# Both branches' first score chunk in one product, and squares summed by ScalarE, in a two-layer decoder trunk

## The chip, the cores and the metric

The kernel runs on one core of one Trainium2 chip. The metric is the device time of one execution in microseconds (us). The profile below is of one execution taken by the hardware profiler; PE is TensorE (PEld its weight loads), ACT is ScalarE, DVE is VectorE, POOL is GpSimd, SP is SyncE, which issues most DMAs.

## What is computed

Two layers over 512 positions of width 1024, all in float32. Layer 0 has one input projection whose columns feed an mLSTM branch (4 heads of 128) and a sparse attention branch (8 query heads of 64 in 2 key/value groups), then one output projection. Layer 1 is a gated linear recurrence (HGRN2, 8 heads of 128) between two projections. Cut to what the change touches:

```python
qh = partial_rope(rms_norm(heads(q, 8), q_norm), pos) * (64 ** -0.5)
ks_h = partial_rope(rms_norm(heads(ks, 2), k_norm[1]), pos)      # selected branch
kw_h = partial_rope(rms_norm(heads(kw, 2), k_norm[2]), pos)      # window branch
...
s_s = q . ks ;  p_s = masked_softmax(s_s) ; o_s = p_s @ vs       # with 8 blocks and top-k 16, all causal keys
s_w = q . kw ;  p_w = masked_softmax(s_w) ; o_w = p_w @ vw       # the window of 512 spans the sequence
out = g0 * o_c + g1 * o_s + g2 * o_w
...
h = rms_norm(h_mlstm, head_norm)      # mLSTM: mean of squares per head of 128
o = rms_norm(o_hgrn2, head_norm)      # HGRN2: the same
```

So the selected and the window branch are both plain causal attention of the same queries over different keys and values, and every head norm needs a sum of squares.

## The kernel before, in words

**Layout.** The 512 positions are four chunks of 128 (`NT = 4`). Large projections run as three products for each float32 one (the high and low parts of both operands, `whi`/`wlo` against `h0h`/`h0l`): ACT rounds a weight block into `whi` and DVE subtracts to give `wlo` (`cvt_w`). These products are the dense work; each streams 512 columns.

**Order.** The code describes work in strands (generators) that a small flow model interleaves in program order: `dense0` and `dense1` go through the projection groups and have the lowest priority, the others (`prep_q`, `prep_k`, `nsa_a`, `nsa_b`, `m_head`, `m_tok`, `hgrn`) are put between their products as their inputs come ready. Then `Plan` takes all operations of a layer with a price for each and places them again by a list schedule (six rounds, the best kept), on all engines. So whatever changes an operation, its price or its buffers changes the order written to every queue. Work buffers come in rings; the tag `big` has 5 (`BB`), counted by `hb(n)` (wait until n are free) and `b_end()` (give one back).

**Queries and keys (`prep_q`, `prep_k`, one call each per chunk).** From the projected rows `qk[i]` (8 heads of q, then 4 of k, 64 columns each) ACT squares all heads in one instruction into `sq`, a block of the tag `big`; POOL multiplies `qk[i]` by the norm weight in place; DVE sums each head's 64 squares (`tensor_reduce` into `qss` or `kss4`); POOL makes the reciprocal root in two instructions (`rsqrt_mean`); DVE scales into `x2` and applies the rotation; PE transposes; ACT and DVE write the high and low parts stacked on the partitions (`q2`) or side by side (`kd[g][:, c, br, :]`, c for high and low, br for the branch).

**Scores (`nsa_a`).** There are 16 units: for each group, pair of heads and branch br (0 selected, 1 window), two heads hh. A unit goes through the four query chunks i: two products (c = 0, 1) of the same queries as weights against `128 * (i + 1)` key columns, into one bank of the tag `sc` (two banks); DVE adds the causal mask and takes the minimum into `nm`; ACT takes the exponential into the unit's row block `PP` with the row sum into `sm`. Then DVE scales each chunk's block by gate over sum. `nsa_b` transposes the blocks on PE (`tp<-cs,PP` in the profile) and multiplies with the values.

**Head norms.** In `m_tok` (4 calls) and in `hgrn` (8 calls) ACT squares four blocks of 128 columns, one instruction each with the sum in `accum_out`. All four write their squares, which nobody reads, to the same scrap block `hj`.

In the profile a matmul is named by output, then moving and weight operands; an ACT instruction with `accum_out` is followed by an ACTIVATION_READ_ACCUMULATOR. All operations are recorded by one helper, so all rows have the line L408 and are told apart by tile names; `x` there is the tile `x2`, `kss` is `kss4`, `krs` is `krs4`, `hj` is also the second layer's `hj1`, and `CUSTOM_DVE_ANT_0` is the masking minimum.

Of the kernel before, what the change touches and what calls it, by code (L numbers as in the profile page):

```python
# [31 lines left out]
NT = 4  # L32
# [583 lines left out]
def build(tc, I, out):  # L616
# [6 lines left out]
    with ExitStack() as ctx:  # L623
# [323 lines left out]
        with ExitStack() as c0:  # L947
# [8 lines left out]
            def hb(n):  # L956
                return lambda: big[0] >= n
# [4 lines left out]
            def b_t(name, shape, dt=F32):  # L962
                big[0] -= 1
                assert big[0] >= 0, name
                return cut(sp.tile([128, 1280], dt, name=name, tag="big", bufs=BB), shape)
# [238 lines left out]
            def turn(x2):  # L1204
# [3 lines left out]
                return cut(p, (4, 128))  # L1208

            def prep_q(i):  # L1210
                yield hb(2)
                x = qk[i][:, :8, :]
                ts_ = slice(128 * i, 128 * (i + 1))
                sq = b_t("sq", (8, 64))
                A.activation(sq, x, AF.Square)
                P.tensor_tensor(x, x, cust(qnB, [[0, 8], [1, 64]]), op=OP.mult)
                ss = s_t("qss", [128, 8])
                V.tensor_reduce(ss, sq, axis=AX.X, op=OP.add)
                b_end()
                rq = s_t("qrs", [128, 8])  # L1220
# [18 lines left out]
            def prep_k(i):  # L1239
                yield hb(2)  # L1240
                x = qk[i][:, 8:, :]
                ts_ = slice(128 * i, 128 * (i + 1))
                sq = b_t("sq", (4, 64))
                A.activation(sq, x, AF.Square)
                P.tensor_tensor(x.rearrange("p (a b) c -> p a b c", a=2), x.rearrange("p (a b) c -> p a b c", a=2),
                                cust(knB, [[64, 2], [0, 2], [1, 64]], 64), op=OP.mult)
                ss = s_t("kss4", [128, 4])
                V.tensor_reduce(ss, sq, axis=AX.X, op=OP.add)
                b_end()
                rk = s_t("krs4", [128, 4])  # L1250
# [55 lines left out]

            def nsa_a():
                yield [E("q%d" % i) for i in range(4)] + [E("k%d" % i) for i in range(4)] + [E("gt")]
                for u, (g, pr, br, hh) in enumerate(UN):
                    hg = 4 * g + 2 * pr + hh  # L1310
                    yield [hb(1), lambda u=u: ndone[0] >= u - 1, SCS]
                    pp = b_t("PP", (1280,))
                    nm = s_t("nm", [128, 4], 3)
                    sm = s_t("sm", [128, 4], 3)
                    for i in range(NT):
                        n = 128 * (i + 1)
                        yield SCS
                        s = sc_t()
                        for c in range(2):
                            T.matmul(s[:, :n], q2[g][:, hh, pr, 128 * i:128 * (i + 1)], kd[g][:, c, br, :n],  # L1320
                                     start=c == 0, stop=c == 1)
                        V.tensor_tensor_reduce(s[:, :n], s[:, :n], cz[:, 512 - n:], 1.0, -NEG, op0=OP.add, op1=OP.min,
                                               accum_out=nm[:, i:i + 1])
                        A.activation(pp[:, OFF[i]:OFF[i] + n], s[:, :n], AF.Exp, bias=nm[:, i:i + 1], scale=-1.0,
                                     accum_out=sm[:, i:i + 1])
                    V.reciprocal(sm, sm)
                    V.tensor_tensor(sm, sm, cust(gt, [[24, 4]], 3 * hg + 1 + br), op=OP.mult)
                    for i in range(NT):
                        sl = slice(OFF[i], OFF[i] + 128 * (i + 1))
                        V.tensor_scalar(pp[:, sl], pp[:, sl], sm[:, i:i + 1], None, op0=OP.mult)  # L1330
                    PPs[u] = pp
                    fl.mark(E("A%d" % u))
                    if u % 8 == 7:
                        u_end(1 + u // 8)
# [3 lines left out]
            def nsa_b():  # L1338
                pts = []
                yp = None  # L1340
                for u, (g, pr, br, hh) in enumerate(UN):
                    yield [E("A%d" % u), hb(1)]
                    pp = PPs.pop(u)
                    ptl = b_t("PT", (1280,))
                    m = []
                    for kbs, o in (((0,), 0), ((1,), 512), ((2, 3), 896)):
# [3 lines left out]
                        for kb in kbs:  # L1350
                            for i in range(kb, NT):
                                T.transpose(tp[:, c:c + 128], pp[:, OFF[i] + 128 * kb:OFF[i] + 128 * (kb + 1)], idf)
                                c += 128
# [133 lines left out]
            def m_tok(t):  # L1487
# [21 lines left out]
                hs = s_t("hs", [128, 4])  # L1509
                hj = s_t("hj", [128, 128], 1)  # L1510
                for h in range(4):
                    A.activation(hj, nd[:, h, :128], AF.Square, scale=rd[:, h:h + 1], accum_out=hs[:, h:h + 1])
                hr = s_t("hr", [128, 4])
# [204 lines left out]
        with ExitStack() as c1:  # L1718
# [60 lines left out]
            def hgrn(h):  # L1779
# [100 lines left out]
                hs = s_t("hs1", [128, 4])  # L1880
                hj = s_t("hj1", [128, 128], 1)
                for t in range(4):
                    A.activation(hj, op[:, 128 * t:128 * (t + 1)], AF.Square, accum_out=hs[:, t:t + 1])
                hr = s_t("hr1", [128, 4])
# [234 lines left out]
```

## Time and profile before

| | before |
|---|---|
| median of three runs | 623.28 us (620.89 to 623.8) |
| the profiled execution | 619.54 us, its span 617.8 us |
| PE busy | 609.2 us (99%) |
| DVE busy | 463.9 us (75%) |
| ACT busy | 326.4 us (53%) |
| POOL busy | 104.5 us (17%) |
| mean granted TensorE clock | 0.997 of full |

Busy time is the share of the span in which an engine had an instruction; matmuls are pipelined and the profile models their ends, so what one of them costs is read from the distance between starts, not from its duration. A timeline merges neighbours of the same kind (x2). In brackets behind a row stands the idle time of the engine before it and what ended it.

### The profile page before, as it was taken

What the parts mean: (1) busy time and instruction counts of PE and PEld (TensorE: products, weight loads), DVE (VectorE), ACT (ScalarE), POOL (GpSimd) and SP (SyncE); (2) the same over time, 40 slices, a digit from 0 to 9 for tenths busy, and PEclk for the clock granted to TensorE, in tenths of its full rate; (3) what the DMA queues carried; (4) which work ended last, traced back from release to release, by engine and by line L of the source; (5) the groups of instructions that cost most, each with busy time, mean ns of one, the idle gap of its engine ahead of it and who ended that gap; (6) DMA issues with size and microseconds to landing.
All of it is one profiled execution on the core that took longest, in us unless ns stands there. A gap on an engine that the chain in (4) does not pass through costs nothing.

```text
span 617.8 us, 11670 instructions
## 1 busy us (share of the span) xinstructions
PE 609.2 (99%) x4498; PEld 492.0 (80%) x4498; DVE 463.9 (75%) x988; ACT 326.4 (53%) x778; POOL 104.5 (17%) x131
## 2 busy tenths in 40 slices
PE   8999998999999999999999999999999999999997
PEld 8877886877777777888888887788877877788886
DVE  5888989988899875656746669997688798986441
ACT  7554433675676765273534757447527375565410
POOL 1424252031100000063003111023000100122100
PEclk9998999999999999999999999999999999999999
DMA  8823137679994004016244424473222215473111
GB/s 293 278 117 103 51 103 256 203 164 342 247 203 138 0 2 147 7 46 228 77 162 136 154 85 138 118 240 121 69 72 69 70 34 173 138 282 128 35 69 68
DMA packets 23526, 82.90 MB, mean 134 GB/s; under 512 B 3376, under 2 KB 4272, under 8 KB 20656
## 3 DMA queue, kind: packets, MB, share of 16 engines
q1 hardware_dynamic: 21168, 65.39, 32.2%
q0 software_dynamic: 2304, 16.78, 10.3%
q8 instruction: 35, 0.57, 0.4%
q14 instruction: 19, 0.16, 0.1%
HBM read 77.96 MB, written 20.97 MB: 160 GB/s over the span
## 4 chain that ended last, share of the span: by engine, by line
PE 92%; DVE 3%; DMA 1%; issue 1%; POOL 1%; ACT 1%; SPq 0%; ACTq 0%; DVEq 0%
PE mm L408 35%; PE mx L408 17%; PE my L408 15%; PE sc L408 8%; PE tp L408 5%; PE ac L408 5%; PE tq L408 5%; PE sd L408 2%; DMA raw<-in_wall_dram 1%; DVE wlo L408 1%; DVE HB L408 0%; DVE AL L408 0%; POOL krs L408 0%; ACT whi L408 0%; DVE x L408 0%
## 5 line engine op out<-in xcount | busy, mean ns | idle before, releaser
L408 ACT ACTIVATE whi<-raw 128x512 fp32r<-128x512 f32 (+1 forms) x184 | 105.0, 614 | 76.2 <-PE my L408 29.5
L408 DVE TENSOR_TENSOR wlo<-raw,whi 128x1024 fp32r<-128x1024 f32 (+1 forms) x96 | 114.7, 1202 | 20.4 <-ACT whi L408 20.1
L408 PE MATMUL mm<-whi,h0h 128*128 128x512 f32 (+1 forms) x168 | 68.2, 407 | 0.0
L408 PE MATMUL mm<-whi,h0l 128*128 128x512 f32 (+1 forms) x168 | 67.9, 405 | 0.0
L408 PE MATMUL mm<-wlo,h0h 128*128 128x512 f32 (+1 forms) x168 | 67.4, 405 | 0.0
L408 ACT ACTIVATE PP<-sc,nm 128x128 f32<-128x128 f32 (+2 forms) x64 | 33.7, 527 | 26.0 <-DVE nm L408 22.9
L408 DVE CUSTOM_DVE_ANT_0 sc<-sc,cz 128x128 f32<-128x128 f32 (+2 forms) x64 | 31.4, 502 | 11.7 <-PE sc L408 9.1
L408 PE MATMUL mm<-h0h,whi 128*128 128x512 f32 x96 | 39.5, 411 | 0.0
L408 PE MATMUL mm<-h0h,wlo 128*128 128x512 f32 x96 | 38.1, 397 | 0.6 <-DVE wlo L408 0.6
L408 PE MATMUL mm<-h0l,whi 128*128 128x512 f32 x96 | 38.6, 402 | 0.0
L408 PEld LDWEIGHTS mm<-whi,h0l 128*128 128x128 f32 x168 | 32.1, 192 | 5.8 <-issue 0.2
L408 PEld LDWEIGHTS mm<-wlo,h0h 128*128 128x128 f32 x168 | 32.2, 192 | 5.6 <-issue 0.2
L408 PEld LDWEIGHTS mm<-whi,h0h 128*128 128x128 f32 x168 | 32.3, 192 | 5.2
L408 DVE TENSOR_TENSOR HB<-HB,tt 128x512 f32<-128x512 f32 x48 | 31.9, 687 | 4.4 <-PE sd L408 3.1
L408 PE MATMUL sc<-kd,q 128*128 128x512 f32 (+3 forms) x128 | 31.3, 330 | 0.0
L408 ACT ACTIVATE PT<-tp 128x384 f32<-128x384 f32 (+1 forms) x48 | 24.0, 526 | 9.5 <-PE tp L408 9.2
L408 POOL TENSOR_TENSOR ivgg<-ivgg,zz 128x256 f32<-128x256 f32 x16 | 17.8, 1116 | 65.9 <-ACT zz L408 65.9
L408 POOL TENSOR_SCALAR hr<-hs 128x4 f32<-128x4 f32 x12 | 2.3, 193 | 142.7 <-ACT hj L408 142.6
L408 PE MATMUL tp<-cs,PP 128*128 128x128 f32 x160 | 26.3, 275 | 0.0
L408 PEld LDWEIGHTS sc<-kd,q 128*128 128x128 f32 x128 | 22.7, 191 | 4.0 <-ACT PT L408 0.8
L408 PE MATMUL my<-h1l,whi 128*128 128x512 f32 x64 | 25.8, 403 | 0.0
L408 PE MATMUL mx<-h1l,whi 128*128 128x512 f32 x64 | 25.8, 402 | 0.0
(374 smaller groups left out, 1556.7 us busy)
## 6 DMA issues: line engine op xcount, KB each, us to landing
raw<-in_wall_dram SPq DMA_DIRECT2D x76, 512.0 KB, 3.8
wt<-in_wall_dram POOLq DMA_DIRECT2D x12, 1024.0 KB, 14.2
raw<-wt SPq DMA_DIRECT2D x16, 512.0 KB, 3.7
wt<-wt POOLq DMA_DIRECT2D x4, 1024.0 KB, 22.7
bias<-in_brow_dram SPq DMA_DIRECT2D x9, 256.0 KB, 4.1
xt<-in_xt_dram SPq DMA_DIRECT2D x8, 256.0 KB, 5.4
w<-in_cw_dram SPq DMA_DIRECT2D x2, 1024.0 KB, 9.4
x<-in_xt_dram SPq DMA_DIRECT2D x2, 1024.0 KB, 6.8
```

Source lines behind the costliest of these rows:

```text
L408: o.fn(*o.a, **k)
```

## The change

Three edits. **Scores:** in `nsa_a` the first chunk (128 keys) of both branches is computed in the unit of branch 0: its two products stream 256 columns (`kd[g][:, c, :, :128]`), DVE and ACT treat the two halves of the bank one after the other, and the window branch's half goes to a tile `e0` (128 columns, three buffers) and to that unit's own `nm1`/`sm1`. The units of branch 1 start at chunk 1. **Squares of q and k:** in place of one ACT instruction over all heads and a DVE reduction, ACT squares one head at a time with `accum_out`, into a scrap tile `sqj` with one block for each head; `sq` and its block of the tag `big` go away, and the strand waits for one free block and not two. **Head norms:** the four squares go to four blocks of a scrap tile (`sqj` in `m_tok`, `hj1` of four times the size in `hgrn`).

```diff
+            def squares(x, ss):
+                j = cut(s_t("sqj", [128, 512], 1), (8, 64))
+                for a in range(x.shape[1]):
+                    A.activation(j[:, a, :], x[:, a, :], AF.Square, accum_out=ss[:, a:a + 1])
             def prep_q(i):
-                yield hb(2)
+                yield hb(1)
...
-                sq = b_t("sq", (8, 64))
-                A.activation(sq, x, AF.Square)
+                ss = s_t("qss", [128, 8])
+                squares(x, ss)
                 P.tensor_tensor(x, x, cust(qnB, [[0, 8], [1, 64]]), op=OP.mult)
-                ss = s_t("qss", [128, 8])
-                V.tensor_reduce(ss, sq, axis=AX.X, op=OP.add)
-                b_end()
                 rq = s_t("qrs", [128, 8])
...
(prep_k: the same with 4 heads)
...
                     pp = b_t("PP", (1280,))
-                    nm = s_t("nm", [128, 4], 3)
-                    sm = s_t("sm", [128, 4], 3)
-                    for i in range(NT):
+                    if br == 0:
+                        for b_ in range(2):
+                            mm_[b_, hh] = s_t(f"nm{b_}", [128, 4], 3), s_t(f"sm{b_}", [128, 4], 3)
+                        first[hh] = s_t("e0", [128, 128], 3)
+                    nm, sm = mm_[br, hh]
+                    def chunk(s, n, i, p, nm, sm):
+                        V.tensor_tensor_reduce(s, s, cz[:, 512 - n:], 1.0, -NEG, op0=OP.add, op1=OP.min,
+                                               accum_out=nm[:, i:i + 1])
+                        A.activation(p, s, AF.Exp, bias=nm[:, i:i + 1], scale=-1.0, accum_out=sm[:, i:i + 1])
+                    for i in range(br, NT):
...
                         for c in range(2):
-                            T.matmul(s[:, :n], q2[g][:, hh, pr, 128 * i:128 * (i + 1)], kd[g][:, c, br, :n],
-                                     start=c == 0, stop=c == 1)
...
+                            T.matmul(s[:, :n] if i else cut(s, (2, 128)), q2[g][:, hh, pr, 128 * i:128 * (i + 1)],
+                                     kd[g][:, c, br, :n] if i else kd[g][:, c, :, :n], start=c == 0, stop=c == 1)
+                        chunk(s[:, :n], n, i, pp[:, OFF[i]:OFF[i] + n], nm, sm)
+                        if i == 0:
+                            chunk(s[:, 128:256], n, i, first[hh], *mm_[1, hh])
...
-                hj = s_t("hj", [128, 128], 1)
+                hj = cut(s_t("sqj", [128, 512], 1), (4, 128))
                 for h in range(4):
-                    A.activation(hj, nd[:, h, :128], AF.Square, scale=rd[:, h:h + 1], accum_out=hs[:, h:h + 1])
+                    A.activation(hj[:, h, :], nd[:, h, :128], AF.Square, scale=rd[:, h:h + 1], accum_out=hs[:, h:h + 1])
...
-                hj = s_t("hj1", [128, 128], 1)
+                hj = s_t("hj1", [128, 4, 128], 1)
                 for t in range(4):
-                    A.activation(hj, op[:, 128 * t:128 * (t + 1)], AF.Square, accum_out=hs[:, t:t + 1])
+                    A.activation(hj[:, t, :], op[:, 128 * t:128 * (t + 1)], AF.Square, accum_out=hs[:, t:t + 1])
```

The rest of the diff takes the first block of a branch 1 unit from `e0` where DVE scales it and PE transposes it.

## Rows read from the trace of the kernel before

**Rows 1.** The page, its first part: busy time of the engines, its share of the span, and the number of instructions.

```profile
PE 609.2 (99%) x4498; PEld 492.0 (80%) x4498; DVE 463.9 (75%) x988; ACT 326.4 (53%) x778; POOL 104.5 (17%) x131
```

**Rows 2.** The page's chain of work that ended last, by engine, as shares of the span.

```profile
PE 92%; DVE 3%; DMA 1%; issue 1%; POOL 1%; ACT 1%; SPq 0%; ACTq 0%; DVEq 0%
```

**Rows 3.** Busy time by stretch: the stretch and its length, then PE, PEld, DVE, ACT and POOL, each with its number of instructions, the granted clock, and the DMA's share and rate. From 36 to 104 us q and k are prepared, from 104 to 235 us `nsa_a` runs, up to 345 us the last projections of layer 0, from 410 to 520 us most of `hgrn`.

```profile
36.00:104.00 68.00, 66.09 (x375) 53.10 (x374) 59.09 (x142) 26.84 (x62) 27.00 (x30) 0.97 0.31 103
...
50.50:54.00 3.50, 3.50 (x10) 2.85 (x10) 2.90 (x7) 0.00 (x0) 0.00 (x0) 0.51 0.11 16
104.00:235.00 131.00, 131.00 (x731) 100.96 (x731) 110.67 (x316) 88.10 (x228) 11.40 (x16) 1.00 0.59 161
235.00:345.00 110.00, 110.00 (x544) 90.17 (x543) 65.21 (x107) 51.61 (x123) 22.71 (x23) 1.00 0.35 117
410.00:520.00 110.00, 109.05 (x1241) 87.43 (x1243) 89.96 (x193) 60.75 (x153) 13.99 (x19) 1.00 0.29 92
```

**Rows 4.** The waits of PE over the span: who waited for whom, us in total, times, the longest.

```profile
PE tp L408 <- DVE kd L408: 1.2, 1, 1.2
...
PE mm L408 <- DVE wlo L408: 0.6, 1, 0.6
...
PE tq L408 <- DVE yo L408: 0.2, 1, 0.2
```

**Rows 5.** Groups of PE instructions with shapes kept apart: the scores' first chunk, its count, busy time and mean duration.

```profile
L408 PE MATMUL sc<-kd,q 128*128 128x128 f32 x32 | 6.6, 267 | 0.0
```

**Rows 6.** The timeline of PE in the scores, where a first and a second chunk of one unit stand between dense products: start, duration.

```profile
110.65 0.33 PE L408 MATMUL sc<-kd,q 128*128 128x128 f32 x2
110.82 0.45 PE L408 MATMUL mm<-h0l,whi 128*128 128x512 f32 x1
111.11 0.39 PE L408 MATMUL mm<-h0h,wlo 128*128 128x512 f32 x1
111.34 0.39 PE L408 MATMUL mm<-h0h,whi 128*128 128x512 f32 x1
...
111.81 0.40 PE L408 MATMUL sc<-kd,q 128*128 128x256 f32 x2
112.05 0.40 PE L408 MATMUL mm<-h0h,wlo 128*128 128x512 f32 x1
112.28 0.39 PE L408 MATMUL mm<-h0h,whi 128*128 128x512 f32 x1
```

**Rows 7.** The tile `sq` from 36 to 96 us: count, shortest, median and longest duration in ns, first and last start.

```profile
L408 ACT ACTIVATE sq<-qk x8: 409/520/632, 37.3 to 90.0; 128x512 f32<-128x512 f32 x4, 128x256 f32<-128x256 f32 x4
L408 DVE TENSOR_REDUCE qss<-sq x4: 668/676/680, 42.4 to 64.5; 128x8 f32<-128x512 f32 x4
L408 DVE TENSOR_REDUCE kss<-sq x4: 405/412/420, 76.9 to 93.9; 128x4 f32<-128x256 f32 x4
```

**Rows 8.** The timeline of ACT at the one square of 64 columns with a sum that the kernel before has (64 partitions).

```profile
47.65 0.26 ACT L408 ACTIVATE kn<-kr 64x64 f32<-64x64 f32 x1 [1.20 <-DVE kr L408]
47.82 0.19 ACT L408 ACTIVATION_READ_ACCUMULATOR kn<-kr 64x1 f32 x1
```

**Rows 9.** The timeline of ACT at two exponentials of a unit in a row: they write different blocks of the tile `PP` and different columns of `sm`.

```profile
107.49 0.37 ACT L408 ACTIVATE PP<-sc,nm 128x128 f32<-128x128 f32 x1 [0.43 <-DVE nm L408]
107.75 0.19 ACT L408 ACTIVATION_READ_ACCUMULATOR PP<-sc,nm 128x1 f32 x1
107.87 0.48 ACT L408 ACTIVATE PP<-sc,nm 128x256 f32<-128x256 f32 x1
```

**Rows 10.** The timeline of ACT at two squares of an `m_tok` head norm; they write the same block `hj`.

```profile
262.10 0.39 ACT L408 ACTIVATE hj<-nd,rd 128x128 f32<-128x128 f32 x1
...
262.61 0.40 ACT L408 ACTIVATE hj<-nd,rd 128x128 f32<-128x128 f32 x1
```

**Rows 11.** The timeline of ACT at two squares of an `hgrn` head norm; they write the same block.

```profile
493.68 0.28 ACT L408 ACTIVATE hj<-tq 128x128 f32<-128x128 f32 x1 [3.86 <-PE tq L408]
493.86 0.19 ACT L408 ACTIVATION_READ_ACCUMULATOR hj<-tq 128x1 f32 x1
494.08 0.28 ACT L408 ACTIVATE hj<-tq 128x128 f32<-128x128 f32 x1
```

**Rows 12.** The timeline of DVE before PE's two longest waits in the preparation of k.

```profile
88.30 1.23 DVE L408 TENSOR_TENSOR wlo<-raw,whi 128x1024 fp32r<-128x1024 f32 x1
...
92.01 1.98 DVE L408 TENSOR_TENSOR wlo<-raw,whi 128x1024 fp32r<-128x1024 f32 x1
93.92 0.41 DVE L408 TENSOR_REDUCE kss<-sq 128x4 f32<-128x256 f32 x1
94.25 0.28 DVE L408 TENSOR_TENSOR r<-x,cs 128x128 f32<-128x128 f32 x1
```

**Rows 13.** The timeline of POOL in the same stretch: the multiplication of k by its norm weight.

```profile
92.15 0.76 POOL L408 TENSOR_TENSOR qk<-qk,knB 128x256 f32<-128x256 f32 x1
```

**Rows 14.** The timeline of PE before and in the stretch of the lower clock: products of four columns, and dense products.

```profile
49.08 0.38 PE L408 MATMUL tp<-cs,rows 4*128 4x4 f32 x2
49.39 0.50 PE L408 MATMUL mm<-wlo,h0h 128*128 128x512 f32 x1
...
52.09 0.63 PE L408 MATMUL mm<-whi,h0h 128*128 128x512 f32 x1
52.52 0.63 PE L408 MATMUL mm<-whi,h0l 128*128 128x512 f32 x1
```

More of the change, by code (lines that the diff above doesn't have):

```diff
@@ L1239, in prep_k @@
             def prep_k(i):
-                yield hb(2)
+                yield hb(1)
                 x = qk[i][:, 8:, :]
                 ts_ = slice(128 * i, 128 * (i + 1))
-                sq = b_t("sq", (4, 64))
-                A.activation(sq, x, AF.Square)
+                ss = s_t("kss4", [128, 4])
+                squares(x, ss)
                 P.tensor_tensor(x.rearrange("p (a b) c -> p a b c", a=2), x.rearrange("p (a b) c -> p a b c", a=2),
                                 cust(knB, [[64, 2], [0, 2], [1, 64]], 64), op=OP.mult)
-                ss = s_t("kss4", [128, 4])
-                V.tensor_reduce(ss, sq, axis=AX.X, op=OP.add)
-                b_end()
                 rk = s_t("krs4", [128, 4])
@@ L1307, in nsa_a @@
             def nsa_a():
+                mm_, first = {}, {}
                 yield [E("q%d" % i) for i in range(4)] + [E("k%d" % i) for i in range(4)] + [E("gt")]
@@ L1319, in nsa_a @@
                         for c in range(2):
-                            T.matmul(s[:, :n], q2[g][:, hh, pr, 128 * i:128 * (i + 1)], kd[g][:, c, br, :n],
-                                     start=c == 0, stop=c == 1)
[L1322 to L1325, printed above, removed]
+                            T.matmul(s[:, :n] if i else cut(s, (2, 128)), q2[g][:, hh, pr, 128 * i:128 * (i + 1)],
[3 more added lines that the diff above has]
+                            chunk(s[:, 128:256], n, i, first[hh], *mm_[1, hh])
                     V.reciprocal(sm, sm)
@@ L1328, in nsa_a @@
                     for i in range(NT):
-                        sl = slice(OFF[i], OFF[i] + 128 * (i + 1))
-                        V.tensor_scalar(pp[:, sl], pp[:, sl], sm[:, i:i + 1], None, op0=OP.mult)
-                    PPs[u] = pp
+                        ps = pp[:, OFF[i]:OFF[i] + 128 * (i + 1)] if i or br == 0 else first[hh]
+                        V.tensor_scalar(ps, ps, sm[:, i:i + 1], None, op0=OP.mult)
+                    PPs[u] = pp, first[hh] if br else pp[:, :128]
                     fl.mark(E("A%d" % u))
@@ L1342, in nsa_b @@
                     yield [E("A%d" % u), hb(1)]
-                    pp = PPs.pop(u)
+                    pp, p0 = PPs.pop(u)
                     ptl = b_t("PT", (1280,))
@@ L1351, in nsa_b @@
                             for i in range(kb, NT):
-                                T.transpose(tp[:, c:c + 128], pp[:, OFF[i] + 128 * kb:OFF[i] + 128 * (kb + 1)], idf)
+                                src = pp[:, OFF[i] + 128 * kb:OFF[i] + 128 * (kb + 1)] if i else p0
+                                T.transpose(tp[:, c:c + 128], src, idf)
                                 c += 128
```

## The prediction

> **What bounds the kernel now.** I read the page first. PE is busy for 609.2 of 617.8 us, DVE for three quarters, ACT for half [rows 1]. A busy PE can still be a waiting one, so the chain of waits comes next: 92% of the span is PE's own work, DVE has 3%, POOL and ACT 1% each [rows 2]. The windows then show the three stretches that the change touches: PE is busy for 66.09 of 68 us while q and k are prepared, for all 131 us of the scores, and for 109.05 of 110 us in most of the second layer's recurrence [rows 3]. Last, the waits of PE: the long ones that the touched code can move are 1.2 us for `kd`, 0.6 us for `wlo` and 0.2 us for `yo` [rows 4]. So the reader is to see a kernel in which PE's instruction count and columns set the time. An edit pays if it takes PE work away, or if it stands in one of these few waits; work of ACT, DVE and POOL is hidden behind dense products unless it comes late.
>
> **Scores.** Before there are 32 products of 128 columns: 16 units, two each [rows 5]. After there are 16 of 256 columns, in the 8 units of branch 0, and none in the others. For the price I take distances between starts. A pair of 128 columns starts at 110.65; the dense product behind it starts 0.17 us later, and the next one 0.29 us after that, where the ordinary distance of dense products is 0.23 us (111.11 to 111.34). So the pair costs 0.17 + 0.29 - 0.23 = 0.23 us [rows 6]. A pair of 256 columns costs 0.24 us (111.81 to 112.05), and the dense product behind it has the ordinary 0.23 us [rows 6]. Double the columns cost the same, so a short product costs what its weight load costs. For two units of the same head the change saves 2 x 0.23 - 0.24 = 0.22 us, and for the 8 such pairs of units 1.76 us; I take **1.7 us**. PE has no idle time in this stretch that this could fall into [rows 3], so it comes off the end. If only the distance up to the next start counted, 2 x 0.17 - 0.24 = 0.10 us would be saved each time, 0.8 us in all. The Trainium skill has a rule that speaks against this edit (TensorE: Matmul & The Clock Gate, section Back-to-back issue gap): the isolated distance grows with the streamed columns, N / 2.4 + 2.5 ns, which would be an estimated 8 x (4 x 56 - 2 x 109) ns, or 0.05 us, saved. The same section says that this form counts too little at small N, because it leaves out the weight load; the rows above agree with that remark and not with the formula.
>
> DVE and ACT do as many minima and exponentials as before; eight of each move from branch 1's unit to branch 0's. The bank of `sc` now serves two minimum-exponential chains one after the other before it is free, so it is held longer by about the distance of one exponential, 0.38 us (107.49 to 107.87), and a minimum [rows 9]. I cost that at nothing: dense products fill PE while a score bank is waited for, and do so through the whole stretch. If that cover were gone it would cost at most 8 x 0.8 = 6.4 us (an estimate, an exponential and a minimum of its length).
>
> **Squares of q and k.** Out go four DVE reductions of 0.676 us and four of 0.412 us, 4.35 us of DVE, and eight ACT squares, four of about 0.63 and four of about 0.41 us, 4.2 us [rows 7]. In come 32 + 16 = 48 ACT squares of 64 columns with a sum. No such row on 128 partitions exists. From below: the one on 64 partitions reads its sum 0.17 us after its start [rows 8], and an exponential follows the sum of the one before it by 0.12 us when they write different blocks [rows 9], together 0.29 us. From above: 0.51 us, the distance of two squares of 128 columns that write one block [rows 10]. The first is nearer, since the new ones write different blocks and are short; I take 0.33 us. That is 2.6 us of ACT for a q chunk in place of 0.63, 1.3 us for a k chunk in place of 0.41, and 48 x 0.33 - 4.2 = 11.6 us more ACT in all (9.7 to 20). ACT is busy for 26.84 of 68 us there [rows 3], so it has the room. POOL's multiplication by the norm weight overwrites what is squared, so it now waits for the last square and not the only one, and the reciprocal root behind it on POOL waits with it; each q chunk comes some 2 us later, each k chunk about 0.5 us. Nobody needs them at that moment: PE is filled to 235 us while the scores run, and for all 110 us from there to 345 us too [rows 3]. I cost the delay at nothing; what it costs without cover is the rival on the slow side.
>
> What it may gain stands in PE's two waits near 94 us, 1.8 us together [rows 4], plus the refill behind them, 2.1 us. DVE was late there: a `wlo` of normally 1.23 us took 1.98 us while POOL multiplied k for 0.76 us from 92.15, and a reduction of k's squares followed at 93.92, which puts what is behind it 0.33 us later (93.92 to 94.25) [rows 12, 13]. The reduction goes: 0.33 us. The Trainium skill (SBUF — State Buffer, section Who interferes with whom) says that a DVE operation with two SBUF inputs and a GpSimd operation that reads SBUF exclude each other for the whole instruction; here the 0.75 us too many are POOL's 0.76. The change keeps POOL's multiplication and moves it behind the squares, so whether the two meet again is even odds: another 0.75 / 2 = 0.37 us. Together I take **0.7 us**, between 0 and 2.1.
>
> **Head norms.** Squares into one block start 0.40 us apart in the recurrence, the next 0.22 us after the sum is read [rows 11]; with separate blocks the follower came 0.12 us after it [rows 9]. So each of three gaps shrinks by 0.10 us, 0.3 us for each of 12 head norms, 3.6 us of ACT. Nearly all of it is hidden behind dense products. PE waited for what follows once visibly, 0.2 us for `yo` [rows 4]. I take **0.1 us**, between 0 and 0.5.
>
> **The new order.** Every price and buffer that changes lets the planner place everything anew. What this can move is seen in one place: from 50.5 to 54 us the clock was granted at 0.51, the level of 1.2 GHz, after PE had alternated between single dense products and products of a few columns (49.08 and 49.39) [rows 3, 14]; some seven dense products, three quarters of that stretch, started 0.43 us apart where 0.23 is normal [rows 14], a loss of 7 x 0.2 = 1.4 us. The order of just that stretch changes (the first q chunks are prepared there), so this may vanish or grow: plus or minus 1.4 us, taken as nothing.
>
> **Sum.** 1.7 + 0.7 + 0.1 = 2.5 us off. The profiled execution took 619.54 us (span 617.8 and 1.7 around it) and would take 617.0. It is 3.7 us under the median of the runs shown; off the median the same sum gives **620.8 us**, 0.4% less. About 0.5% is what a measurement of this kernel can tell from no change.
>
> **Rivals.**
> *Columns set the price.* If a product's distance to the next start is all that it costs, the scores give 0.8 us and not 1.7: 623.28 - 0.8 - 0.8 = 621.7 us. The 0.29 us behind the short pair speak against it. This includes the formula of the skill's page, by which the scores would give nothing and the time would be 622.5.
> *The new order removes the stalls.* Scores 1.7, both waits near 94 us 2.1, the low clock 1.4, `yo` and its like 0.5: 5.7 us off, 617.6 us. For it: DVE, the engine that was late there, loses 4.35 of its 59.09 us [rows 3] and ACT, which takes the work, was the idler one. Against it: the waits stem from single collisions that a new order can also make.
> *ScalarE stands in front of the weights.* Each weight block needs two ACT roundings before DVE and PE can have it, and ACT works in order. If a run of eight squares lands before a rounding that is due, PE waits for the difference, 2.6 - 0.63 = 2 us; for all four q chunks 8 us, with the gains of 2.5 taken off: 623.28 + 8 - 2.5 = 628.8 us. It decides from the point at which weights are ready less than 2 us ahead of use. For it: `wlo` was late once already. Against it: it was late through DVE, and ACT idled for 60% of the stretch.
> *The separate blocks free nothing.* If the distance of the squares comes from reading the sum and not from the shared block, the head norms stay and the new squares cost up to 0.51 us; hidden as well, so 620.9 us. It can't be told from the forecast by time, only by the rows.
>
> **How the numbers follow.** Forecast (with the last rival, which has its time): 0.48. Stalls removed: 0.25. Columns set the price: 0.11. ScalarE in front: 0.16, which stands also for other ways in which a new order makes new waits. The likeliest time is 620.8. The low end, 616.5, lies a little under the rival at 617.6; the high end, 626.5, takes in new waits of up to half of the slow rival's 8 us on top of the sum, and the spread of the runs shown. Faster by over 0.5% needs under 620.16: nearly all of the second case and a quarter of the forecast's, 0.36. Slower by over 0.5% (above 626.4) is most of the last case, 0.14. Within: 0.50.
>
> **What would show it.** Right: 16 score products of 256 columns more and 32 of 128 fewer, dense distance 0.23 us behind them; 48 squares about 0.33 us apart; no waits of PE for `whi` or for the low parts near 36 to 104 us; head norm squares 0.29 us apart; the span shorter by PE's products alone. Wrong: PE waiting for `wlo` with ACT busy on squares; score banks late and PE idle from 104 to 235 us; a second stretch at the lower clock; or distances of 0.40 us still between squares of separate blocks.

## The result and the profile after

The changed kernel takes **624.23 us** (median of 21 runs, 622.06 to 626.01); the kernel before takes 619.96 us in as many runs beside it (618.21 to 624.37). The ratio is **1.0063, interval 1.0050 to 1.0077**: slower by 0.6%, where 0.4% less was forecast. The profiled execution took 623.38 us, its span 621.6 us.

The page of the changed kernel, busy time and the chain of work that ended last:

```profile
PE 606.8 (98%) x4482; PEld 489.2 (79%) x4482; DVE 456.7 (73%) x980; ACT 328.9 (53%) x866; POOL 103.0 (17%) x131
...
PE 86%; DVE 5%; DMA 5%; issue 1%; ACT 1%; POOL 1%; SPq 0%; ACTq 0%; DVEq 0%; POOLq 0%
```

PE is busy for 2.4 us less than in [rows 1], but the span is longer, and the chain has lost 6% of PE and holds 5% of DMA where it held 1% [rows 2]. So time went from work to waiting. PE's waits say which:

```profile
PE tp L408 <- ACT PT L408: 4.7, 1, 4.7
PE sc L408 <- ACT whi L408: 2.3, 2, 1.2
PE tq L408 <- ACT kT L408: 1.1, 1, 1.1
...
PE tp L408 <- DVE kd L408: 0.8, 1, 0.8
```

The wait for `wlo` of [rows 4] is gone and that for `kd` is down from 1.2 us, as forecast. A single wait of 4.7 us is new, and one of 1.1 us for `kT` in the second layer. The wait of `sc` for `whi` falls before 40 us, where the kernel before waits 0.9 us; nothing is read from it, since it lies between 0.5 and 2.1 us in executions of kernels that have the first 100 us in the order of the kernel before (before_late and before_lag, below, are the two ends). By stretch (columns as in [rows 3]; the last one is inside the second):

```profile
36.00:104.00 68.00, 66.80 (x389) 53.79 (x388) 57.32 (x154) 37.67 (x161) 25.94 (x29) 1.00 0.32 103
104.00:235.00 131.00, 126.33 (x683) 97.53 (x683) 103.18 (x294) 82.67 (x217) 12.04 (x18) 0.97 0.59 161
...
149.80:154.50 4.70, 4.70 (x13) 3.60 (x13) 2.09 (x6) 3.59 (x9) 0.00 (x0) 0.50 1.02 250
```

The preparation of q and k has no low clock in this execution (1.00, 0.97 before). That is not the new order's doing: from 48 to 56 us the granted clock is 0.79 in the profiles of before and before_late, but 1.00 in those of before_gated and before_lag, in which PE, ACT and DVE go through the first 100 us in the same order. The loss is in the scores, where PE was busy for all 131 us. The chain there, in order of time (start, length):

```profile
136.78 1.08 DVE wlo L408
137.85 0.03 DVE sm L408
137.88 10.58 DMA raw<-in_wall_dram
...
148.54 0.04 ACT whi L408
...
149.08 0.59 ACT PT L408
...
149.71 0.90 PE tp L408 x3
```

A weight block that was issued at 137.88 landed 10.58 us later. ACT, which takes its instructions in order, stood at the rounding of that block, as its timeline shows:

```profile
141.19 1.15 ACT L408 ACTIVATE whi<-raw 128x512 fp32r<-128x512 f32 x2
148.54 0.63 ACT L408 ACTIVATE whi<-raw 128x512 fp32r<-128x512 f32 x1 [6.20 <-DMA raw<-in_wall_dram]
149.08 0.96 ACT L408 ACTIVATE PT<-tp 128x512 f32<-128x512 f32 x2
```

Behind it stands `PT`, the copy that empties the bank of the transposed scores. PE, in order as well, needs that bank, with dense products that could have filled the gap queued behind:

```profile
144.06 0.99 PE L408 MATMUL sc<-kd,q 128*128 128x384 f32 x4
149.71 0.90 PE L408 MATMUL tp<-cs,PP 128*128 128x128 f32 x3 [4.67 <-ACT PT L408]
...
150.84 0.63 PE L408 MATMUL mm<-h0l,whi 128*128 128x512 f32 x1
151.27 0.63 PE L408 MATMUL mm<-h0h,wlo 128*128 128x512 f32 x1
```

After the idle 4.7 us the dense products start 0.42 to 0.43 us apart: the clock is granted at 0.50, the level of 1.2 GHz, to 154.5 us. Half of 4.70 us is 2.35 us; with the wait that is 7.0 us lost in one place.

What shares the DMA engines is seen on POOL's timeline, here in the changed kernel and then in the kernel before:

```profile
114.06 1.45 POOL L408 TENSOR_SCALAR th<-th 128x512 f32<-128x512 f32 x2 [8.76 <-ACT th L408]
115.47 4.36 POOL L408 DMA_DIRECT2D wt<-in_wall_dram  x7
```

```profile
126.05 4.11 POOL L408 DMA_DIRECT2D wt<-in_wall_dram  x6
```

`wt` are 16 background transfers of 1 MB (`presums`, `sums`, `Adds.put`) that add pairs of the second layer's weight blocks in DRAM. A due time in the planner places them, but in the program nothing holds back those that have no earlier transfer to wait for, except POOL's order. In the kernel before the burst follows `th` at 126 us; here `th` came 11 us earlier and the burst with it. The list of DMA issues has for the block of 137.88:

```profile
raw<-in_wall_dram SPq DMA_DIRECT2D x1, 512.0 KB, 10.6
```

and for the four blocks from 189 to 200 us, behind the transfers, a median of 3.6 us. The planner prices a block as 1.125 us plus its bytes at 360 per ns, 2.6 us in all (`schedule`, `Loads`). So the order is a consistent plan for loads that land 2.6 us after their issue.

### The profile page after: what moved, and what is told of

It is laid out like the page before. It is cut to its first block, busy times and chain, and to the rows that moved or that the text cites. A ratio compares the mean times of both kernels' runs of the same rounds, so it can differ in the third digit from the quotient of the medians.

```text
span 621.6 us, 11725 instructions
## 1 busy us (share of the span) xinstructions
PE 606.8 (98%) x4482; PEld 489.2 (79%) x4482; DVE 456.7 (73%) x980; ACT 328.9 (53%) x866; POOL 103.0 (17%) x131
## 4 chain that ended last, share of the span: by engine, by line
PE 86%; DVE 5%; DMA 5%; issue 1%; ACT 1%; POOL 1%; SPq 0%; ACTq 0%; DVEq 0%; POOLq 0%
PE mm L408 33%; PE mx L408 16%; PE my L408 14%; PE sc L408 7%; PE tp L408 5%; PE ac L408 5%; PE tq L408 5%; DMA raw<-in_wall_dram 3%; PE sd L408 2%; DVE wlo L408 2%; DMA xt<-in_xt_dram 1%; DMA raw<-wt 1%; ACT whi L408 1%; DVE HB L408 1%; DVE ivgg L408 1%
## 5 line engine op out<-in xcount | busy, mean ns | idle before, releaser
L408 ACT ACTIVATE PP<-sc,nm 128x256 f32<-128x256 f32 (+3 forms) x56 | 30.7, 551 | 27.7 <-DVE nm L408 26.8
L408 DVE CUSTOM_DVE_ANT_0 sc<-sc,cz 128x512 f32<-128x512 f32 (+3 forms) x64 | 31.1, 503 | 13.9 <-PE sc L408 11.1
L408 PE MATMUL mm<-h0h,wlo 128*128 128x512 f32 x96 | 39.5, 411 | 0.0
L408 PE MATMUL tp<-cs,PP 128*128 128x128 f32 x152 | 23.9, 276 | 4.7 <-ACT PT L408 4.7
L408 PE MATMUL sc<-kd,q 128*128 128x256 f32 (+2 forms) x112 | 28.4, 345 | 0.0
L408 POOL TENSOR_TENSOR ivgg<-ivgg,zz 128x256 f32<-128x256 f32 x16 | 16.3, 1020 | 68.7 <-ACT zz L408 68.7
L408 PEld LDWEIGHTS tp<-cs,PP 128*128 128x128 f32 x152 | 19.0, 142 | 9.9 <-ACT PT L408 5.3
L408 PE MATMUL my<-h1h,whi 128*128 128x512 f32 x64 | 25.8, 403 | 0.0
```

The costliest lines, as they stand in the source:

```text
L408: o.fn(*o.a, **k)
```

## The experiments

**Theory:** the new order has ACT round a weight block soon after its issue and ahead of `PT`; the block is late because the transfers share its engines; ACT and PE, both in order, stop. **Rivals:** the changed computation itself, ScalarE's squares above all, starves PE; or the transfers do, wherever the rounding stands.

| kernel | median, us | ratio to before (interval) |
|---|---|---|
| after_small | 615.51 | 0.9948 (0.9927 to 0.9969) |
| before_small | 619.74 | 1.0006 (0.9992 to 1.0019) |
| after_late | 622.67 | 1.0062 (1.0039 to 1.0084) |
| before_late | 624.32 | 1.0077 (1.0060 to 1.0093) |
| after_chain | 627.39 | 1.0105 (1.0078 to 1.0133) |
| scores | 619.88 | 0.9997 (0.9980 to 1.0014) |
| squares | 624.91 | 1.0074 (1.0048 to 1.0100) |
| heads | 619.52 | 0.9995 (0.9976 to 1.0015) |
| after_gated | 622.70 | 1.0040 (1.0019 to 1.0061) |
| before_gated | 625.69 | 1.0103 (1.0073 to 1.0133) |
| scores_small | 619.89 | 1.0004 (0.9987 to 1.0021) |
| squares_small | 620.09 | 1.0004 (0.9988 to 1.0019) |
| heads_small | 619.81 | 1.0009 (0.9990 to 1.0028) |
| after_lag | 617.02 | 0.9954 (0.9935 to 0.9973) |
| after_lag10 | 616.31 | 0.9948 (0.9929 to 0.9966) |
| before_lag | 619.26 | 0.9985 (0.9971 to 0.9999) |
| squares_lag | 620.23 | 0.9992 (0.9972 to 1.0013) |
| scores_lag | 619.27 | 0.9996 (0.9978 to 1.0014) |

### The transfers cut to an eighth

```diff
-        self.plan.add("P", self.eng.dma_start, (out, src), k, 1000.0)
+        self.plan.add("P", self.eng.dma_start, (out[:, :256], src[:, :256]), k, 1000.0)
...
-                return wt[q][:, 2048 * c + o:2048 * c + o + 1024]
+                return wblock(f"r{2 * q}", c)[:, o:o + 1024]
```

This version leaves the sums out: the second layer reads weight blocks that are not summed, so its output is another one. PE, ACT and DVE keep their orders.

> The changed kernel with the 16 background transfers that build the second layer's weight sums cut to an eighth of their columns (that layer then reads unsummed blocks, so this part of the computation is left out). PE, ACT, DVE orders are those of the changed kernel. Theory (these transfers delay a weight block, ACT waits for it in order, PE behind ACT for 4.8 us, and the clock falls after that): no such wait, ACT's 6.2 us wait for the weight block near 148 us gone, time 616.0 to 617.7 us, ratio to the kernel before 0.993 to 0.997. Rival (the 48 squares on ScalarE, or the two chains on one score bank, make PE late): 624 us as the changed kernel.

> The kernel before with the same cut of the background transfers (the weight sums are left out in the same way), orders of PE, ACT and DVE as before. Theory: no PE wait of before hung on these transfers, so 620 us, ratio 0.997 to 1.003. Rival (the transfers slow whatever runs beside them, in both kernels alike): faster by the same 7 us as the changed kernel, 613 us.

The changed kernel lost its long wait and went to 0.9948; the kernel before did not move. Weight blocks issued from 137 to 150 us in after_small:

```profile
raw<-in_wall_dram SPq DMA_DIRECT2D x4, 512.0 KB, 3.4
```

So the same order is faster than the kernel before if the blocks land in time. The changed computation does not starve PE by itself.

### The transfers issued later, or chained

after_late and before_late:

```diff
-PS = 95000.0, 10500.0
+PS = 165000.0, 7000.0
```

after_chain:

```diff
-            steps = [(t3, wblock(b, 0), 0), (t2, wblock(a, 0), 0), (t3, wblock(b, 1), 1), (t4, wblock(a, 1), 0),
-                     (t1, wblock(a, 0), 0), (t2, t3, 1), (t1, wblock(b, 0), 1), (t4, t2, 1)]
+            steps = [(t3, wblock(b, 0), 0), (t3, wblock(b, 1), 1), (t2, wblock(a, 0), 0), (t2, t3, 1),
+                     (t4, wblock(a, 1), 0), (t4, t2, 1), (t1, wblock(a, 0), 0), (t1, wblock(b, 0), 1)]
...
-                    sums(n % 2, n // 2)
+                    sums(n // 8, n % 8)
```

> The changed kernel with the background transfers complete but planned from 165 us on, 7 us apart, in place of 95 us and 10.5 us; the orders of PE, ACT, DVE and of the weight loads are those of the changed kernel. Theory: the weight blocks near 140 us land in 4 us, no PE wait of over 1 us near 145 us, 616 to 618 us, ratio 0.993 to 0.997, unless the later blocks near 190 us are delayed instead. Rival (squares or score banks): 624 us.

> The kernel before with the same later background transfers, other orders as before. Theory: 620 us, ratio 0.997 to 1.003, since its weight blocks near 141 to 153 us landed in 10 to 16 us without a wait of PE. Rival (transfers slow both alike): 613 to 615 us.

> The changed kernel, complete, with the background transfers put in an order in which nearly each one adds to the one before and so waits for its landing: two or three are on their way at a time, not seven. Orders of PE, ACT, DVE and of the weight loads are those of the changed kernel. Theory (the burst of seven makes the weight block late): the block issued near 138 us lands in 4 to 7 us in place of 10.6, the wait of PE near 145 us is under 1.5 us, the clock stays up, 616 to 619 us, ratio 0.994 to 0.998. Rival (ACT's order itself is late there): the wait stays, 622 to 624 us.

after_late missed: the due times do not hold the transfers on the chip, they still went out from 115 us, a block of 137.64 took 10.2 us and PE waited 4.3 us for `PT`. before_late missed too, and is the useful one. There the transfers lasted to 200 us and met other blocks, and the kernel before fell into the same trap with its own computation; ACT in before_late:

```profile
190.44 1.14 ACT L408 ACTIVATE whi<-raw 128x512 fp32r<-128x512 f32 x2
195.63 1.15 ACT L408 ACTIVATE whi<-raw 128x512 fp32r<-128x512 f32 x2 [4.05 <-DMA raw<-in_wall_dram]
```

after_chain tested whether it takes the burst of seven. It does not: with two or three transfers in flight where the block is issued PE waits twice, and the time is above both the forecast and its rival. PE's waits in after_chain:

```profile
PE tp L408 <- ACT PT L408: 7.1, 2, 4.1
```

### Each edit alone

scores is the kernel before with the hunks of `nsa_a` and `nsa_b`, squares with `squares`, `prep_q` and `prep_k`, heads with the scrap blocks of `m_tok` and `hgrn`; a line of each:

```diff
+                                     kd[g][:, c, br, :n] if i else kd[g][:, c, :, :n], start=c == 0, stop=c == 1)
...
+                squares(x, ss)
...
+                    A.activation(hj[:, h, :], nd[:, h, :128], AF.Square, scale=rd[:, h:h + 1], accum_out=hs[:, h:h + 1])
```

> Of the change the scores alone (first chunk of both branches in one product). Prediction's term: 1.7 us less, 618.2 us against 620. Theory: that, plus a wait of PE of some us with the lower clock if the new order's weight blocks meet the transfers in the scores' stretch; without one 617.5 to 619. Rival (two chains on one score bank hold PE up): PE waits for score banks, slower than before.

> Of the change the squares of q and k alone. Prediction's term: 0.7 us less (0 to 2.1), 619.3 us against 620. Theory: that, and a long wait only where a weight block meets the transfers. Rival (ScalarE stands in front of the weights): PE waits for weights near 36 to 104 us with ACT on squares, up to 8 us slower.

> Of the change the head norms alone. Prediction's term: 0.1 us less (0 to 0.5), 619.9 us against 620, ratio 0.998 to 1.001; squares of one head norm 0.26 us apart in place of 0.40. It leaves POOL's and the weight loads' orders as before, so no new collision is expected.

Only the squares are slower, by as much as all three; the scores gain nothing where 1.7 us less was forecast. ACT in squares:

```profile
146.86 0.50 ACT L408 ACTIVATE PT<-tp 128x384 f32<-128x384 f32 x1
153.30 1.15 ACT L408 ACTIVATE whi<-raw 128x512 fp32r<-128x512 f32 x2 [5.94 <-DMA raw<-in_wall_dram]
```

The same wait, on another block (issued at 141.62, it took 11.6 us); PE waited 2.9 us for an exponential behind it, whose score bank it needed. The squares themselves are done some 60 us earlier; what is left of them there is their effect on the order.

### The transfers held back

Each transfer gets a one-column copy on POOL ahead of it, which reads an output of a dense group behind the scores (`mv`, `mo`, `mz`, `o00`); in the plan the transfer follows that copy:

```diff
-        k = {"_ns": ns, "_after": next(o for o in reversed(self.plan.ops) if o.eng == "T")}
+        k = {"_ns": ns, "_after": self.plan.ops[-1]}
...
                         self.evac(j, pp[j])
+                        names = ("mv", "mo", "mz", "o00")
+                        if self.name in names:
+                            n_ = 4 * names.index(self.name) + j
+                            src = vx[0][:, j, 0, :1] if n_ < 4 else gz[j][:, :1] if n_ < 12 else x1[0][:, j, :1]
+                            P.tensor_copy(hm[:, 15:16], src)
+                            sums(n_ % 2, n_ // 2)
...
-            fl.add(presums(), 0)
```

> All three edits, full transfers, but each of the 16 background transfers that pre-sum the second layer's weights has a one-column copy on POOL ahead of it that reads an output of a dense group behind the scores; so they can only go out there, one by one. The order of PE and ACT through the scores is that of the changed kernel. Collision theory (a weight block is late because the transfers share its engines): no transfer before some 230 us, weight blocks of the scores stretch land in 3 to 5 us, PE's 4.7 us wait before the transposition of the scores is gone, no low clock behind it; 614 to 618 us, ratio 0.992 to 0.997. Rival (the new order itself starves PE, whatever the transfers do): the wait stays above 3 us and the time stays at 622 to 624 us, ratio about 1.005. A third outcome: the transfers now meet the weight blocks of layer 0's last projections, with waits of PE there, 619 to 624 us.

> The kernel before with the same gates. Collision theory: it had no long wait of PE in the scores, so it gains little or nothing, 618 to 620 us, ratio 0.997 to 1.001, and the changed kernel with gates is below it by 3 to 5 us. Rival (the gates help both kernels alike, so the change itself is what is slow): it gains as much as the changed kernel does and stays below it.

The third outcome came, and before_gated came at 625.69 us where at most 620 was expected. In the scores PE waits for nothing, though its order there is unchanged; but now the blocks of the layer's end are late. ACT in after_gated:

```profile
341.19 1.15 ACT L408 ACTIVATE whi<-raw 128x512 fp32r<-128x512 f32 x2 [1.63 <-PE mm L408]
347.06 0.63 ACT L408 ACTIVATE whi<-raw 128x512 fp32r<-128x512 f32 x1 [4.72 <-DMA raw<-in_wall_dram]
```

The loss goes where the transfers go. The kernel before waits there too (2.6 us in one wait); in both profiles PE is idle for 3.5 of the 175 us from 235 to 410 us. It ends 3.0 us behind the changed kernel.

### The edits alone with small transfers

The edits of "Each edit alone" together with that of "The transfers cut to an eighth".

> The score edit alone, with the background transfers cut to an eighth of their columns (the second layer reads weight blocks that are not summed, so its output is another one). Compared with the kernel before cut in the same way, 619.74 us. If the prediction's term is right, 1.7 us less, 618.0 us; if columns set the price, 0.8 less, 618.9; if the new order takes stalls away as well, under 617.5.

> The squares of q and k alone, with the background transfers cut to an eighth of their columns (the second layer reads weight blocks that are not summed). Compared with 619.74 us. By the prediction's term 0.7 us less, 619.0 us, or down to 2.1 less if both waits near 94 us and the low clock near 52 us go (617 to 618); with the run of eight squares in front of the weight roundings as the rival has it, more than 620.5.

> The head norms' edit alone, with the background transfers cut to an eighth of their columns (the second layer reads weight blocks that are not summed). Compared with the kernel before cut in the same way, 619.74 us, from which all three edits took 4.2 us. By the prediction's term 0.1 us less, 619.6 us; if the head norms stand on the path of the second layer's recurrence, up to 3.6 us less, 616.

Without the collision the squares lose nothing, but no edit alone gains anything that can be measured. The three together gain 4.2 us (615.51 against 619.74).

### The planner told when a block lands

```diff
-                x.done = xfer
+                x.done = xfer + (7000.0 if 105000.0 < t < 215000.0 else 0.0)
```

10000.0 in after_lag10. The stretch is the one in which the traces show late blocks. Nothing that is computed or transferred changes, only the order.

> The changed kernel, all transfers and computation as they are; the planner alone is told that a weight block issued between 105 and 215 us lands 7 us later than it believed (it believes some 2.6 us, the traces show 10 to 17 there). ACT then has the transposed scores ahead of the third block's rounding at the place of the long wait. If the cause is the place that the order gave to a block whose load is priced as if nothing else were on the DMA engines: PE's 4.7 us wait for the transposed scores goes, no low clock behind it, transfers still go out from about 115 us, 615 to 619 us, ratio 0.993 to 0.999. If the transfers starve PE wherever the rounding stands: another wait of over 3 us between 115 and 200 us, 621 to 625 us.

> The same with 10 us in place of 7, which gives another order again from about 150 us on. If the cause is the believed landing time, it comes out like 7 us, 615 to 619.5 us with no wait of over 2 us in the scores; if the gain of 7 us were luck of one order, the two differ by more than 3 us.

> The kernel before with the same 7 us. It had no long wait in the scores, so it should stay at 618 to 621 us, ratio 0.998 to 1.003; the changed kernel with 7 us is then below it by about the 3 to 4 us that the two pairs without the collision differ by. If the later landing alone helps any order, it falls to 616 us or less.

> The squares of q and k alone, with the planner told that a weight block issued between 105 and 215 us lands 7 us later. Alone they were slower (624.91 us) with one long wait of ACT for a weight block at 153 us. If that had the same cause as in the changed kernel: no such wait, 617 to 620 us, ratio 0.994 to 1.0, of which the prediction's term alone would give 618.6 (0.7 under the 619.26 of the kernel before with the same 7 us). If the squares starve PE by ScalarE's extra work itself: 622 us or more.

> The score edit alone with the same 7 us, against 619.26 us for the kernel before with it. By the prediction's term 1.7 us less, 617.6 us; if the new order of the second layer gives part of it back (a wait of PE for kT as in all kernels with the score edit), 618 to 619.

This settles it. In after_lag10 SP issues the same block at 137.56, from the same burst of transfers, and it is as late:

```profile
raw<-in_wall_dram SPq DMA_DIRECT2D x1, 512.0 KB, 11.0
```

But ACT has `PT` ahead of the third block's rounding, which now stands at 151.45 (its timeline):

```profile
140.87 1.15 ACT L408 ACTIVATE whi<-raw 128x512 fp32r<-128x512 f32 x2
142.74 0.98 ACT L408 ACTIVATE PT<-tp 128x512 f32<-128x512 f32 x2 [0.72 <-PE tp L408]
```

and PE goes from the scores to the transposes and on to dense products (its timeline):

```profile
143.73 0.99 PE L408 MATMUL sc<-kd,q 128*128 128x384 f32 x4
144.56 0.49 PE L408 MATMUL tp<-cs,PP 128*128 128x128 f32 x3
144.81 0.48 PE L408 MATMUL mm<-h0h,whi 128*128 128x512 f32 x1
```

The same 20 us (columns as in [rows 3]) in the changed kernel:

```profile
140.00:160.00 20.00, 15.33 (x69) 10.86 (x68) 11.71 (x26) 6.56 (x15) 1.63 (x2) 0.83 1.02 270
```

and in after_lag10:

```profile
140.00:160.00 20.00, 20.00 (x107) 15.46 (x105) 17.74 (x44) 12.13 (x31) 1.62 (x2) 1.00 1.02 267
```

The DMA engines are as full in both; PE does 107 instructions in place of 69. The rows of PE, ACT, DVE and POOL follow one another as in the changed kernel up to this rounding, which is the first of ACT's that has moved, so its place is what made the wait. The time falls from 1.0063 to 0.9948 of the kernel before, 7.1 us, against the 7.0 us read off the trace. This version beats both kernels. after_lag gains as much; its profiled execution, 621.81 us, is the slowest of its twelve, but PE waits for nothing from 104 to 235 us there either. before_lag moves little (0.9985), as it had no long wait. squares_lag has no long wait in the scores either and is back at 0.9992, so the squares alone were slow for this reason too.

## Why the prediction was wrong

**What bounds the kernel**: right. PE does, and what was added to its waits was added to the time.

**The step that failed** is "The new order", taken as nothing within 1.4 us, and with it the cover on which "Nobody needs them at that moment" and "I cost the delay at nothing" rest. The reasoning asked who waits for the moved results and found dense products as cover. It did not ask which place a load's consumer gets on an engine that works in order. The cover failed because PE's order is fixed: the dense products stood behind the transpose that waited. It cost 7.0 us in the trace, and after_lag10 gave 7.1 us back, where 1.4 was the bound; and those 1.4 us belong to an execution, not to an order: the same order has the low clock near 52 us or does not. That the later q and k chunks had a part in the 7.0 us is not shown. `th` and the burst moved too, but they stand as early in after_lag10, which does not lose by them.

The trace of the kernel before had the warning. Its block of 141.08, beside the same transfers, was as late (its list of DMA issues):

```profile
raw<-in_wall_dram SPq DMA_DIRECT2D x1, 512.0 KB, 9.6
```

It landed at 150.68. With three `raw` buffers (`RB`) it is the block that ACT rounds at 150.74, after 0.35 us without work (ACT's timeline):

```profile
146.48 1.15 ACT L408 ACTIVATE whi<-raw 128x512 fp32r<-128x512 f32 x2
...
150.74 1.15 ACT L408 ACTIVATE whi<-raw 128x512 fp32r<-128x512 f32 x2 [0.35 <-PE mm L408]
```

Between these two roundings ACT has exponentials and gates to do; in the changed kernel the rounding of the late block stands right behind the one before it. So the kernel before escaped the wait by its order, and narrowly.

**Scores, 1.7 us**: the mechanism and the size are right in PE's rows. PE's timeline of the changed kernel:

```profile
111.97 0.39 PE L408 MATMUL mm<-h0h,wlo 128*128 128x512 f32 x1
112.20 0.40 PE L408 MATMUL sc<-kd,q 128*128 128x256 f32 x2
112.44 0.40 PE L408 MATMUL mm<-h0h,whi 128*128 128x512 f32 x1
112.67 0.39 PE L408 MATMUL mm<-h0l,whi 128*128 128x512 f32 x1
```

A pair takes 0.24 us with 0.23 behind it, and eight pairs are gone, so "columns set the price" is out for PE's work. In time the edit alone does not show it: 1.7 us would be 0.9973, below all three intervals. The kernels with this edit have the wait for `kT` in the second layer, 1.2 us in scores, 0.5 in scores_small, 1.0 in scores_lag, where ACT shows that it too is a rounding that waits for its block ahead of what PE needs:

```profile
552.93 0.63 ACT L408 ACTIVATE whi<-raw 128x512 fp32r<-128x512 f32 x1 [2.07 <-DMA raw<-in_wall_dram]
...
554.41 0.87 ACT L408 ACTIVATE kT<-tq 128x384 f32<-128x384 f32 x2
```

That takes back 0.5 to 1.2 of the 1.7 us; where the rest goes stays open. The score bank held longer cost nothing, as forecast: in the changed kernel no long wait of PE is for one.

**Squares, 0.7 us**: the waits near 94 us fell from 1.8 to 0.8 us in the changed kernel, the right direction and nearly the size. The price of a square was mis-sized: ACT's timeline of the changed kernel, first for q, then in a head norm of the recurrence,

```profile
37.73 0.24 ACT L408 ACTIVATE sqj<-qk 128x64 f32<-128x64 f32 x1
...
37.96 0.24 ACT L408 ACTIVATE sqj<-qk 128x64 f32<-128x64 f32 x1
...
496.18 0.28 ACT L408 ACTIVATE hj<-tq 128x128 f32<-128x128 f32 x1 [3.40 <-PE tq L408]
...
496.44 0.27 ACT L408 ACTIVATE hj<-tq 128x128 f32<-128x128 f32 x1
```

has 0.23 to 0.24 us from one to the next, not 0.33, below the lower bound of 0.29. By that price they add 48 x 0.24 - 4.2 = 7.3 us of ACT and not 11.6; with the squares alone ACT is busy for 333.2 us in place of 326.4. (The 10.8 us more from 36 to 104 us in the changed kernel hold other work that the new order moved there.) **Head norms, 0.1 us**: squares stand 0.25 to 0.26 us apart, 0.30 was forecast and 0.40 was before, so the rival "separate blocks free nothing" is out; in time nothing shows (0.9995).

**The sum** of 2.5 us less is near what the change is worth where the long wait of the scores is out of both kernels: the pairs differ by 4.2 us (small), 3.0 (gated, where both wait at the layer's end) and 2.2 (7 us, where 3 to 4 were expected). It is not the sum of the three edits alone, which give nothing each. Squares alone have new waits of PE, 1.1 us each, for `x` near 68 us and `vp` near 100 us, which all three together don't have; beyond that it stays open where the parts lose what the whole gains.

**The rivals**: "ScalarE stands in front of the weights" had the sign and the engine that works in order, but named the squares as what stands in front. It was the reverse: a weight rounding, waiting for its load, stood in front of the scores. Its 0.16 stood "also for other ways in which a new order makes new waits", and this is one of those. **The base**: the median of three runs, 623.28 us, was high; with 21 it is 619.96, which would have put the forecast at 617.5.

## What to carry to other kernels

When an edit makes a scheduler place everything anew, look for loads whose real landing time is far from the planner's price and for the first instruction behind their consumers on each engine that works in order; that, not the edit's own work, can set the sign. Background transfers that only another engine's order holds back move whenever that engine's work moves. If a re-planned kernel comes out slower, repair the planner's price before giving up the edit: here that turned 1.0063 into 0.9948.

## What was not expected of the hardware

A block of 512 KB lands in 3.3 to 3.6 us (medians) without the 1 MB transfers and in 10.6 us beside the burst of them; two in flight do nearly the same, 8.8 us as the median of the three blocks issued from 105 to 117 us in after_chain. The Trainium skill (DMA: Bandwidth & Descriptors, section Queues, rings and completion order) says that each DMA engine takes turns between the queues with work, a packet at a time. By that alone a block would take an estimated 2 x 3.4 = 6.8 us beside one other queue, however many transfers wait in it, if packets of both take equally long; the trace agrees that the number matters little, but 10.6 us is three times and not twice. Where the rest goes is seen in the DMA queues of the changed kernel (packets, MB, share of the 16 engines; q0 has the transfers, q1 the blocks). From 137.88 to 141.90 us, with no row for q1:

```profile
q0 software_dynamic: 192, 1.39, 101.1%
```

and from 141.90 us to the landing at 148.46:

```profile
q0 software_dynamic: 170, 1.24, 73.4%
q1 hardware_dynamic: 172, 0.64, 28.4%
```

For 4.0 us after its issue the block moves no packet, while the transfers fill the engines; in after_small the first packet moves 1.0 us after the issue. From there on the two queues move packets nearly one for one, so the trace agrees with the turns, and this takes 6.6 us, near the estimate. Why the first packet waits for 4.0 us is not shown.
